# A two-block network on one core: the filter's decay as one channel tile times a factor per position, and the first layer's expert matrices in transfers of 2 MB, 1 MB and 1 MB

## The chip, the cores and the metric

The kernel runs on one core of a Trainium2 chip. The metric is the device time of one execution in microseconds (us); lower is better. Before the change the median of three runs is 2303.51 us (2303.2 to 2305.22).

The core has a tensor engine (PE; its weight loads are listed as PEld), a vector engine (DVE), a scalar engine (ACT), GpSimd (POOL) and SyncE (SP). SP issues nearly all weight loads and POOL the small loads and the stores to DRAM. Each engine works through its own instructions in a fixed order and waits on semaphores for the others. Sixteen DMA engines carry out what SP and POOL issue.

## What is computed

Two blocks follow each other. The first has two layers; each has a token mixer and a mixture of 16 experts, and the first layer runs them on two streams of 256 tokens (context `hc` and latents `x`), the second on the latents alone. The second block is a Hyena layer and an attention layer. What matters here is the expert part and the Hyena filter:

```python
# first block, each layer and stream; cap = 2 * 256 / 16 = 32 tokens per expert
gate, idx = lax.top_k(jnp.swapaxes(aff, 1, 2), cap)
xs = xn[bidx, idx]
hid = silu(einsum('becd,edf->becf', xs, w_gate)) * einsum('becd,edf->becf', xs, w_up)
ys = einsum('becf,efd->becd', hid, w_down) * gate[..., None]      # then added back at idx
# second block: the Hyena filter, L = 256 positions t in [0, 1], 2048 channels
deltas = abs(linspace(MIN_DECAY, MAX_DECAY, 2048))
decay = exp(-t * deltas[None, :])
hf, hb = h[:, :2048] * decay, h[:, 2048:] * decay
k = concatenate([hf, zeros, hb[:0:-1]]); k = k / sum(abs(k))
```

Each expert matrix (gate, up, down) is 1024 x 1024 float32, 4 MB; a layer has 48 of them. `deltas` rises linearly over the channels.

## The kernel before

**Experts.** `route_tokens` picks the tokens and gathers them into `XS`, `experts` goes through the 16 experts: 8 steps of the contraction (k = 0 to 7) for the gate matrix, 8 for up, then silu and the product (ACT, then DVE L874), four transposes on PE (L877), 8 steps for down. In the first layer a step is two matmuls of 64 x 512 side by side (`expert_k`, L841), so a matrix is 16 matmuls, and the profile has two records for each. Expert 0's gate matrix (`early`, tile `psm`) is woven into the gathering (L816). Every fourth expert the results are scattered back by eight matmuls and added to `hc` and `x` (L895, L898).

**Where the matrices land.** `ew` takes a tile for every two k, 1 MB, and issues its load on SP (L915). In the first layer ten buffers rotate: five called `W` (the buffers that every other weight of the kernel uses too), four `W2`, one `W3`. A load waits until PE has used what the buffer held.

**Filter kernels.** Beside the first layer's experts `hkernels` computes the Hyena filter of the second block: `hfilter` (a small network with three sines), then `hkernel` for 16 tiles of 128 channels. Each of them loads `fw4`, its own 128 KB decay tile (L971, POOL) and `dsk`, runs 4 + 4 + 8 small matmuls (L979, L985, L998), multiplies by the decay on DVE (L980) and stores the result to DRAM (`Kd`).

**What follows.** `experts` is followed by the second layer's mixer: the norm of `hc` and `x`, transposes of the normed tiles `xh` (of `hc`) and `og` (of `x`) on PE (L258), then projections in three passes (L111, L112, L113). Its first loads into `W` are `cum` twice, `wT`, and tiles of `w_ada`. The latter belong to a product that is spread through the mixer (`ada`, L205, four matmuls for each 1 MB tile). The five `W` buffers are held back by `wgate`: a tiny POOL copy (L96) reads expert 15's hidden tile before the buffer may be loaded.

**Order.** The program is written in the order above; the tile scheduler then sets the order of the instructions on each engine by its own timeline model, with tiles handed out per pool. So a change of tile sizes can move instructions that it does not mention.

Of the kernel before, what the change touches and what calls it, by code (L numbers as in the profile page):

```python
# [13 lines left out]
OP = mybir.AluOpType  # L14
# [18 lines left out]
class K:  # L33
# [869 lines left out]

    def ew(self, w, k, dma, ns):

        if k % 2 == 0:
            self.ecount += 1
            r = (self.ecount - 1) % 10 if ns == 2 else 11 - self.ecount
            if ns == 1 and r >= 5:
                t = self.T([128, 2, 1024], "W2", 6)  # L910
            elif r < 5:
                t = self.W([128, 2, 1024])
            else:
                t = self.T([128, 2, 1024], *(("W2", 4) if r < 9 else ("W3", 1)))
            dma(t, w[k // 2].rearrange("p (k n) -> p k n", k=2))  # L915
            self.et = t
        return self.et[:, k % 2]


    def hfilter(self):  # L920
# [32 lines left out]
    def hkernels(self):  # L953

        self.fd = self.T([128, 2, 512], "fd")
        self.nc.gpsimd.dma_start(self.fd, self.A["fd"].rearrange("p (k n) -> p k n", k=2))
        with self.pool("filt", tags=("fc", "fz0", "fw1", "fw2", "fa", "fn", "fh")):
            self.hfilter()
        for g in range(16):
            Kt = self.hkernel(g)  # L960
            self.nc.gpsimd.dma_start(self.Kd[g], Kt.rearrange("p a b c -> p (a b c)"))

    def hkernel(self, ct):

        nc, A, T = self.nc, self.A, self.T
        c0 = 128 * ct
        w4 = T([64, 2, 128], "fw4", 1)
        for i in range(2):
            nc.gpsimd.dma_start(w4[:, i], A["hy_fw4_2"][0, :, 2048 * i + c0:2048 * i + c0 + 128])
        dec = T([128, 2, 128], "dec", 1)  # L970
        nc.gpsimd.dma_start(dec, A["decay"][ct].rearrange("p (t n) -> p t n", t=2))  # L971
        dsk = T([1, 128], "dsk", 1)
        nc.gpsimd.dma_start(dsk, A["hy_d_2"][0:1, c0:c0 + 128])
        a = T([128, 2, 2, 128], "ka", 1)
        ab = T([128, 2, 2, 128], "kb", 1)
        ps = self.P([128, 2, 2, 128], "ad")
        for t in range(2):
            for i in range(2):
                nc.tensor.matmul(ps[:, i, t], lhsT=self.h3[:, t * 128:(t + 1) * 128], rhs=w4[:, i], start=True, stop=True)  # L979
        nc.vector.tensor_tensor(a, ps, dec[:, None].to_broadcast([128, 2, 2, 128]), op=OP.mult)  # L980
        nc.vector.memset(a[0:1, 1, 0, :], 0.0)
        nc.vector.scalar_tensor_tensor(ab, a, -1.0, a, op0=OP.mult, op1=OP.max)
        pn = self.P([128, 128], "ad")
        for i in range(4):
            nc.tensor.matmul(pn, lhsT=self.ones, rhs=ab[:, i // 2, i % 2], start=(i == 0), stop=(i == 3))  # L985
        rn = T([128, 128], "krn", 1)
        nc.vector.reciprocal(rn, pn)
        nc.vector.tensor_tensor(ab[:, 0], a[:, 0], a[:, 1], op=OP.add)
        nc.vector.tensor_tensor(ab[:, 1], a[:, 0], a[:, 1], op=OP.subtract)
        abv = ab.rearrange("p i t n -> p (i t) n")  # L990
        nc.vector.scalar_tensor_tensor(abv, abv, 1.0 / 256, rn[:, None, :].to_broadcast([128, 4, 128]), op0=OP.mult, op1=OP.mult)
        nc.vector.tensor_tensor(ab[0:1, 0, 0, :], ab[0:1, 0, 0, :], dsk, op=OP.add)
        Kt = T([128, 2, 2, 128], "Kt", 2)
        ps = self.P([128, 2, 2, 128], "ad")
        for i in range(2):
            for f in range(2):
                for t in range(2):
                    nc.tensor.matmul(ps[:, i, f], lhsT=self.fd[:, t, i * 256 + f * 128:i * 256 + (f + 1) * 128], rhs=ab[:, i, t],  # L998
                                     start=(t == 0), stop=(t == 1))
        self.copy(Kt, ps)  # L1000
        return Kt
# [466 lines left out]
def _constants():  # L1468
    f8 = np.float64
    c = {}  # L1470
    cf = np.zeros((128, 328), np.float32)
    cf[:, 0:128] = np.eye(128)
    cf[:, 128:256] = 1.0 / 256
    for j in range(4):
        for s in range(2):
            cf[32 * j + s, 256 + 2 * j + s] = 1.0
        for e in range(16):
            cf[32 * j + e, 264 + e] = 1.0
        for h in range(4):
            cf[32 * j + h, 280 + 4 * j + h] = -1.0  # L1480
    cf[:, 296:328] = np.arange(1, 33)
    c["cf"] = cf
    t = np.arange(256)
    perm = (t % 64) * 4 + t // 64
    idx = [255 - t, 255 - perm, t, perm]
    cb = np.zeros((128, 384 + 2048), np.float32)
    cb[:, 0:128] = np.eye(128)
    cb[:, 128:256] = np.triu(np.ones((128, 128)), 1)
    cb[:, 256:384] = 1.0
    cum = np.zeros((128, 2, 8, 256), np.float32)  # L1490
    i = np.arange(256)
    for j in range(4):
        mask = np.where(idx[j][:, None] >= idx[j][None, :], 0.0, NEG)
        cb[:, 384 + 512 * j:384 + 512 * (j + 1)] = mask.reshape(2, 128, 256).transpose(1, 0, 2).reshape(128, 512)
        p = (idx[j][:, None] == i[None, :]).reshape(2, 128, 256).transpose(1, 0, 2)
        q = (idx[j][:, None] >= i[None, :]).reshape(2, 128, 256).transpose(1, 0, 2)
        cum[:, :, j] = p
        cum[:, :, 4 + j] = q
    import ml_dtypes
    c["cb"] = cb[:, :384].astype(ml_dtypes.bfloat16)  # L1500
    c["mask"] = cb[:, 384:].astype(ml_dtypes.bfloat16)
    c["cum"] = cum.reshape(128, -1)
    th = 2 * np.pi * (np.outer(t, t) % 256) / 256
    four = np.concatenate([np.cos(th), np.sin(th)], 1)
    c["four"] = four.reshape(2, 128, 512).transpose(1, 0, 2).reshape(128, -1)
    u = np.arange(64)
    ph = 2 * np.pi * (np.outer(u, u) % 64) / 64
    ch = np.zeros((128, 2, 128), f8)
    for g in range(2):
        ch[64 * g:64 * g + 64, 0, 64 * g:64 * g + 64] = np.cos(ph) / 128  # L1510
        ch[64 * g:64 * g + 64, 1, 64 * g:64 * g + 64] = -np.sin(ph) / 128
    c["chan"] = ch.reshape(128, -1)
    wf = 2 * np.pi * ((np.outer(t, 2 * t + 1)) % 1024) / 1024
    fd = np.concatenate([np.cos(wf), np.sin(wf)], 1)
    c["fd"] = fd.reshape(2, 128, 512).transpose(1, 0, 2).reshape(128, -1)

    ws = 2 * np.pi * (np.outer(2 * t - 255, 2 * t + 1) % 2048) / 2048
    c["fe"] = np.concatenate([np.cos(ws[:128]), np.sin(ws[:128])], 1)
    fi = np.concatenate([np.cos(ws).T, np.sin(ws).T], 0) * (2.0 / 512)
    c["fi"] = fi.reshape(4, 128, 256).transpose(1, 0, 2).reshape(128, -1)  # L1520
    tl = np.linspace(0.0, 1.0, 256).astype(np.float32)
    w = (np.float32(2.0 * math.pi) * t.astype(np.float32) / np.float32(256)).astype(np.float32)
    fr = np.linspace(1e-4, 15, 16).astype(np.float32)
    arg = (fr[None, :] * w[:, None]).astype(np.float32).astype(f8)
    z = np.concatenate([tl[:, None].astype(f8), np.cos(arg), -np.sin(arg)], 1)
    c["zpos"] = z.T
    mind, maxd = math.log(1e-2) / 1.5, math.log(1e-2) / 0.3
    deltas = np.abs(np.linspace(mind, maxd, 2048)).astype(np.float32)
    dec = np.exp(-(tl[:, None] * deltas[None, :]).astype(np.float32).astype(f8))
    c["decay"] = dec.reshape(2, 128, 16, 128).transpose(2, 1, 0, 3).reshape(16, 128, 256)  # L1530
    inv = 1.0 / (10000.0 ** (np.arange(0, 64, 2) / 64.0))
    ra = (t // 64)[:, None] * inv[None, :]
    ca = (t % 64)[:, None] * inv[None, :]
    cs = np.concatenate([np.cos(ra), np.cos(ra), np.cos(ca), np.cos(ca)], 1)
    sn = np.concatenate([-np.sin(ra), np.sin(ra), -np.sin(ca), np.sin(ca)], 1)
    rope = np.stack([cs, sn], 0).reshape(2, 2, 128, 128).transpose(2, 0, 1, 3)
    c["rope"] = rope.reshape(128, -1)
    return {k: np.ascontiguousarray(v if v.dtype.itemsize == 2 else v.astype(np.float32)) for k, v in c.items()}


def _layout(inp):
    a = _constants()
    g = {k: np.asarray(v) for k, v in inp.items()}
# [34 lines left out]
    w = g["w_in"]  # L1578
# [7 lines left out]
        a[n] = g[n]  # L1586
    for n in ("w_e_gate", "w_e_up", "w_e_down"):

        a[n] = g[n].reshape(2, 16, 4, 2, 128, 1024).transpose(0, 1, 2, 4, 3, 5).reshape(2, 16, 4, 128, 2048)
    h = g["hy_w_in_2"][0].reshape(8, 128, 4, 16, 128)[:, :, [1, 2, 0, 3]]  # L1590
    a["hyw"] = h.transpose(3, 1, 2, 0, 4).reshape(16, 128, 4096)
    z = g["at_w_in_2"][0][:, 3072:].reshape(8, 128, 4, 4, 128)
# [8 lines left out]
    q, k = g["at_q_g_2"][0], g["at_k_g_2"][0]  # L1601
# [22 lines left out]
```

## Time and profile before

| | |
|---|---|
| median of 3 runs | 2303.51 us |
| the profiled execution | 2303.25 us, of which its span is 2301.1 us |
| PE, DVE, ACT, POOL busy | 91%, 54%, 32%, 8% of the span |
| DMA | 664.09 MB, mean 289 GB/s |
| first layer's experts | about 372 to 883 us of the span |
| second layer's mixer | from there to about 1150 us, DMA at about half |

The page gives the busy share of each engine over the whole span. For this change the stretch of the first layer's experts and the 25 us behind it matter; there both PE and the DMA engines are nearly always busy, and the question at each point is who waits for whom.

### The profile page before, as it was taken

To read this page: it belongs to the slowest core of one execution; us is meant where nothing else is said; L and a number is where in the kernel's file an instruction comes from. 1 tells how busy PE (TensorE), PEld (TensorE's weight loads), DVE (VectorE), ACT (ScalarE), POOL (GpSimd) and SP (SyncE) were. 2 spreads that over 40 slices of the span, in tenths; PEclk is the share of its full clock that TensorE was granted. 3 is DMA by queue.
4 is the path that set the end of the run, shared out by engine and by line. 5 is a ranking of instruction groups with operands and counts; after the bars stand their busy time and mean duration, and the time that the engine had idled before them with its cause. 6 is when DMAs were issued, how large, how long until landed. Compare 5 with 4: busy or idle time off the path is not lost. (4 is left out here: it accounts for less than half of the span.)

```text
span 2301.1 us, 35032 instructions
## 1 busy us (share of the span) xinstructions
PE 2104.5 (91%) x13956; PEld 1414.4 (61%) x13966; DVE 1250.2 (54%) x2533; ACT 738.7 (32%) x1414; POOL 187.6 (8%) x315
## 2 busy tenths in 40 slices
PE   5999988999999998999779889989988999999998
PEld 3775664334333344765446566565657989979786
DVE  3964544333332425844444545444448888775776
ACT  3323432000000004343222222222225555555665
POOL 1000000011001000000000010010001200110100
PEclk9999999999999999999889999999999999999999
DMA  9247563999999997556799999999995555445320
GB/s 351 101 138 303 212 228 129 401 415 413 416 415 415 412 417 287 197 220 217 290 414 419 417 419 416 412 420 416 419 406 177 171 164 174 155 156 181 119 92 19
DMA packets 129587, 664.09 MB, mean 289 GB/s; under 512 B 12666, under 2 KB 23429, under 8 KB 62352
## 3 DMA queue, kind: packets, MB, share of 16 engines
q1 hardware_dynamic: 115616, 602.89, 67.2%
q0 software_dynamic: 13808, 58.96, 6.5%
q8 instruction: 110, 1.80, 0.3%
q14 instruction: 53, 0.43, 0.1%
HBM read 656.56 MB, written 5.24 MB: 288 GB/s over the span
## 5 line engine op out<-in xcount | busy, mean ns | idle before, releaser
L841 PE MATMUL pmm<-W,XS 128*32 128x256 f32 (+1 forms) x3040 | 371.5, 464 | 31.7 <-DMA W<-in_w_e_gate 22.0
L107 DVE TENSOR_TENSOR lo<-W,hi 128x512 fp32r<-128x512 f32 (+1 forms) x420 | 284.0, 681 | 184.4 <-ACT hi L106 181.5
L106 ACT CAST hi<-W 128x512 fp32r<-128x512 f32 (+1 forms) x420 | 255.5, 612 | 348.0 <-PE pmm L112 157.8
L841 PEld LDWEIGHTS pmm<-W,XS 128*32 128x32 f32 (+1 forms) x3040 | 124.2, 120 | 222.6 <-issue 147.1
L107 DVE TENSOR_TENSOR lo<-Wb,hi 128x512 fp32r<-128x512 f32 x160 | 110.7, 693 | 219.9 <-ACT hi L106 217.4
L841 PE MATMUL pmm<-W,hT 128*32 128x256 f32 (+1 forms) x1536 | 185.9, 461 | 26.3 <-DMA W<-in_w_e_down 9.8
L106 ACT CAST hi<-Wb 128x512 fp32r<-128x512 f32 x160 | 98.7, 619 | 339.8 <-PE pmm L112 278.7
L111 PE MATMUL pmm<-hyx,hi 128*128 128x256 f32 x640 | 194.4, 304 | 0.2 <-DVE rtmp L715 0.2
L113 PE MATMUL pmm<-hyx,lo 128*128 128x256 f32 x640 | 182.5, 285 | 0.8 <-DVE lo L107 0.7
L112 PE MATMUL pmm<-hyx,hi 128*128 128x256 f32 x640 | 181.0, 283 | 0.0
L111 PEld LDWEIGHTS pmm<-hyx,hi 128*128 128x128 f32 x640 | 121.3, 190 | 48.9 <-issue 28.2
L111 PE MATMUL pmm<-hyl,hi 128*128 128x256 f32 x512 | 144.6, 283 | 6.2 <-ACT hi L106 4.5
L112 PE MATMUL pmm<-hyl,hi 128*128 128x256 f32 x512 | 144.1, 282 | 0.0
L113 PE MATMUL pmm<-hyl,lo 128*128 128x256 f32 x512 | 142.8, 283 | 0.0
L841 PEld LDWEIGHTS pmm<-W,hT 128*32 128x32 f32 (+1 forms) x1536 | 62.5, 119 | 117.0 <-issue 62.0
L889 DVE TENSOR_TENSOR Y<-pmm,gt 32x512 f32<-32x512 f32 (+1 forms) x128 | 70.9, 554 | 112.8 <-PE pmm L841 111.0
L113 PEld LDWEIGHTS pmm<-hyx,lo 128*128 128x128 f32 x640 | 121.7, 190 | 3.5 <-issue 1.5
L112 PEld LDWEIGHTS pmm<-hyx,hi 128*128 128x128 f32 x640 | 121.7, 190 | 1.0 <-issue 1.0
L205 PE MATMUL pad<-W,cpad 128*32 128x512 f32 x576 | 92.0, 647 | 23.2 <-DMA W<-in_w_ada 16.9
L871 ACT ACTIVATE h<-pmm 128x256 f32<-128x256 f32 (+1 forms) x31 | 15.1, 488 | 270.7 <-PE pmm L841 270.7
L111 PEld LDWEIGHTS pmm<-hyl,hi 128*128 128x128 f32 x512 | 97.3, 190 | 7.6 <-ACT hi L106 5.6
L112 PEld LDWEIGHTS pmm<-hyl,hi 128*128 128x128 f32 x512 | 97.2, 190 | 0.0
(516 smaller groups left out, 3984.5 us busy)
## 6 DMA issues: line engine op xcount, KB each, us to landing
W<-in_w_e_gate SPq DMA_DIRECT2D x128, 1024.0 KB, 13.9
W<-in_w_e_up SPq DMA_DIRECT2D x128, 1024.0 KB, 14.3
W<-in_w_e_down SPq DMA_DIRECT2D x128, 1024.0 KB, 14.5
W<-in_w_ada SPq DMA_DIRECT2D x48, 1024.0 KB, 6.6
W<-in_hyw SPq DMA_DIRECT2D x32, 1024.0 KB, 5.1
Wb<-in_hyw POOLq DMA_DIRECT2D x30, 1024.0 KB, 10.0
W<-in_ada_w SPq DMA_DIRECT2D x24, 1024.0 KB, 5.3
W<-in_at_w_in SPq DMA_DIRECT2D x16, 1024.0 KB, 5.0
```

The costliest lines, as they stand in the source:

```text
L106: self.nc.scalar.copy(hi, w)
L107: self.nc.vector.tensor_tensor(lo, w, hi.bitcast(F32), op=OP.subtract)
L111: first = mm(out, lhsT=l[0], rhs=r[0], start=start, stop=False)
L112: mm(out, lhsT=l[0], rhs=r[1], start=False, stop=False)
L113: mm(out, lhsT=l[1], rhs=r[0], start=False, stop=stop)
L205: nc.tensor.matmul(ps[32 * j:32 * j + 32, :], lhsT=self.cpad[:, blk, k0 + k, :], rhs=wt[:, k, j * 512:(j + 1) * 512], start=(k0 + k == 0), ...
L841: last = self.nc.tensor.matmul(ps[M * j:M * j + M], lhsT=v, rhs=wt[:, j * N:(j + 1) * N], start=(k == 0), stop=(k == 7))
L871: nc.scalar.activation(hv, pgu[0], AF.Silu)
L889: nc.vector.tensor_tensor(Y[s][32 * r:32 * r + 32, c], py[p0:p0 + 32], gt[s][p0:p0 + 32, c], op=OP.mult)
```

## The change

Two things change. First, `decay` for channel tile `ct` is written as the decay of channel tile 0 (`dec`, 128 x 2 x 128) times a factor that depends on position and tile alone (`dect`, one column per tile). Both are loaded once, before the filter network, and the product on DVE becomes two instructions (one for each half of the positions) that multiply by the factor and by `dec`. Second, in the first layer k = 0 to 3 of a matrix come as one transfer of 2 MB into one of two `W2` buffers, and k = 4, 5 and k = 6, 7 as 1 MB each into `W` (five buffers) or, every sixth time, `W3`. The bytes of the ten buffers are the same. The host lays the matrices out so that each transfer is contiguous; in the first layer a partition's row of the 2 MB transfer is 16 KB, of the others 8 KB. The second layer keeps transfers of 1 MB.

```diff
     def ew(self, w, k, dma, ns):
 
-        if k % 2 == 0:
-            self.ecount += 1
-            r = (self.ecount - 1) % 10 if ns == 2 else 11 - self.ecount
-            if ns == 1 and r >= 5:
-                t = self.T([128, 2, 1024], "W2", 6)
-            elif r < 5:
-                t = self.W([128, 2, 1024])
+        per = 4 if ns == 2 and k < 4 else 2
+        if k % per == 0:
+            if per == 4:
+                t = self.T([128, 4, 1024], "W2", 2)
             else:
-                t = self.T([128, 2, 1024], *(("W2", 4) if r < 9 else ("W3", 1)))
-            dma(t, w[k // 2].rearrange("p (k n) -> p k n", k=2))
+                self.ecount += 1
+                if ns == 1:
+                    t = self.T([128, 2, 1024], "W2", 6) if self.ecount <= 6 else self.W([128, 2, 1024])
+                else:
+                    t = self.T([128, 2, 1024], "W3", 1) if self.ecount % 6 == 0 else self.W([128, 2, 1024])
+            dma(t, w[k * 131072:(k + per) * 131072].rearrange("(p k n) -> p k n", p=128, k=per))
             self.et = t
-        return self.et[:, k % 2]
+        return self.et[:, k % per]
...
+        self.dec, self.dect = self.T([128, 2, 128], "dec"), self.T([128, 2, 16], "dect")
+        self.nc.gpsimd.dma_start(self.dec, self.A["decay"].rearrange("p (t n) -> p t n", t=2))
+        self.nc.gpsimd.dma_start(self.dect, self.A["dect"].rearrange("p (t n) -> p t n", t=2))
...
-        dec = T([128, 2, 128], "dec", 1)
-        nc.gpsimd.dma_start(dec, A["decay"][ct].rearrange("p (t n) -> p t n", t=2))
...
-        nc.vector.tensor_tensor(a, ps, dec[:, None].to_broadcast([128, 2, 2, 128]), op=OP.mult)
+
+        for t in range(2):
+            nc.vector.scalar_tensor_tensor(a[:, :, t], ps[:, :, t], self.dect[:, t, ct:ct + 1],
+                                           self.dec[:, None, t].to_broadcast([128, 2, 128]), op0=OP.mult, op1=OP.mult)
...
-    c["decay"] = dec.reshape(2, 128, 16, 128).transpose(2, 1, 0, 3).reshape(16, 128, 256)
+    c["decay"] = dec[:, :128].reshape(2, 128, 128).transpose(1, 0, 2).reshape(128, 256)
+    step = np.exp(-tl[:, None].astype(f8) * (deltas[None, ::128] - deltas[0]).astype(f8))
+    c["dect"] = step.reshape(2, 128, 16).transpose(1, 0, 2).reshape(128, 32)
```

The change moves instructions in three places that the prediction speaks of. The first is SP's order of loads for expert 13 (any expert from 3 on looks alike). Rows name the line, the tile and its source; 128x2048 is 1 MB, 128x4096 is 2 MB, and the waits are on earlier DMAs (DMAHW) and on PE. Before:

```order
L915 DMA W_4219<-in_w_e_gate 128x2048 [waits DMAHW4_49,PE_49]
L915 DMA W_4225<-in_w_e_gate 128x2048 [waits DMAHW5_49,PE_49]
L915 DMA W_4231<-in_w_e_gate 128x2048 [waits DMAHW6_49,PE_49]
L915 DMA W_4237<-in_w_e_gate 128x2048 [waits DMAHW7_49,PE_49]
L915 DMA W<-in_w_e_up 128x2048 [waits DMAHW0_49,PE_49]
L915 DMA W<-in_w_e_up 128x2048 [waits DMAHW1_49,PE_49]
```

and of the changed kernel:

```order
L916 DMA W<-in_w_e_gate 128x2048 [waits DMAHW5_49,PE_49]
L916 DMA W<-in_w_e_gate 128x2048 [waits PE_49]
L916 DMA W_4141<-in_w_e_gate 128x4096 [waits DMAHW7_49,DMAHW1_49,PE_49]
L916 DMA W<-in_w_e_up 128x2048 [waits DMAHW0_49,PE_49]
L916 DMA W<-in_w_e_up 128x2048 [waits PE_49]
L916 DMA W_4164<-in_w_e_up 128x4096 [waits DMAHW4_49,DMAHW2_49,PE_49]
```

The quarters of a matrix came in the order in which PE uses them. Now the two 1 MB pieces (k = 4 to 7) are issued first and the 2 MB piece, which PE uses first, last.

The second is PE's order behind expert 15's last matmuls: the scatter (L895), the `w_ada` steps (L205) and the transposes of the mixer (L258). Before:

```order
L841 MATMUL pmm<-W,hT 64x512 x8
L895 MATMUL psm<-Y,SgT 128x512 x8
L205 MATMUL pad<-W,cpad 32x512 x4
L258 MATMUL pmm<-cf,xh 128x128 x3
L258 MATMUL ptp<-cf,xh 128x128
L205 MATMUL pad<-W,cpad 32x512 x4
L258 MATMUL pmm<-cf,xh 128x128 x9
L258 MATMUL ptp<-cf,xh 128x128 x3
L258 MATMUL psm<-cf,og 128x128 x2
```

and of the changed kernel:

```order
L841 MATMUL pmm<-W_4379,hT 64x512 x4
L895 MATMUL psm<-Y,SgT 128x512 x2
L205 MATMUL pad<-W,cpad 32x512 x4
L895 MATMUL psm<-Y,SgT 128x512 x2
L205 MATMUL pad<-W,cpad 32x512 x4
L895 MATMUL psm<-Y,SgT 128x512 x4
L205 MATMUL pad<-W,cpad 32x512 x4
L258 MATMUL pmm<-cf,xh 128x128 x3
L258 MATMUL ptp<-cf,xh 128x128
L258 MATMUL pmm<-cf,xh 128x128 x9
L258 MATMUL ptp<-cf,xh 128x128 x3
L205 MATMUL pad<-W,cpad 32x512 x4
```

Four `w_ada` steps instead of two now stand ahead of the transposes of `og`; the third and fourth came from the projections behind, where they stood after 7 and 36 matmuls.

The third is SP's order at the same place, where those steps' tiles are loaded. Before:

```order
L367 DMA W<-in_cum 128x2048 [waits DMAHW1_49,Pool_49]
L377 DMA W<-in_wT 128x2x1024 [waits DMAHW2_49,Pool_49]
L200 DMA W<-in_w_ada 128x2048 [waits DMAHW6_49,DMAHW3_49,Pool_49]
L200 DMA W<-in_w_ada 128x2048 [waits DMAHW7_49,DMAHW4_49,Pool_49]
L485 DMA maskb<-in_mask 128x2048 [waits DMAHW5_49,Pool_49]
```

and of the changed kernel:

```order
L377 DMA W<-in_wT 128x2x1024 [waits DMAHW2_49,Pool_49]
L200 DMA W<-in_w_ada 128x2048 [waits DMAHW3_49,Pool_49]
L200 DMA W<-in_w_ada 128x2048 [waits DMAHW5_49,DMAHW4_49,Pool_49]
L377 DMA W<-in_wT 128x2x1024 [waits DMAHW3_49,PE_49]
L200 DMA W<-in_w_ada 128x2048 [waits DMAHW6_49,DMAHW4_49,PE_49]
L485 DMA maskb<-in_mask 128x2048 [waits DMAHW7_49,Pool_49]
```

The second `wT` tile and the third `w_ada` tile moved ahead of `maskb`; both wait for PE, that is for the first and the second `w_ada` step, whose buffers they take. The fourth tile takes the third's.

The filter kernels' matmuls also moved: of the 16 groups of transposes between up and down (L877), 5 had other work directly before them on PE, now 14 have.

## Rows read from the trace of the kernel before

**Rows 1.** The page's DMA issues: KB each, median us from issue to landing, mixer's `w_ada` kind.

```profile
W<-in_ada_w SPq DMA_DIRECT2D x24, 1024.0 KB, 5.3
```

**Rows 2.** Stretches of the experts: us, busy us (instructions), PEclk, DMA share, GB/s.

```profile
450.00:650.00 200.00, 188.69 (x914) 77.01 (x908) 68.25 (x115) 8.28 (x14) 20.48 (x38) 1.00 1.01 416
650.00:850.00 200.00, 186.24 (x924) 77.79 (x924) 64.82 (x110) 8.27 (x14) 19.93 (x37) 0.99 1.01 414
850.00:871.00 21.00, 18.85 (x97) 7.57 (x92) 5.40 (x9) 0.60 (x1) 1.02 (x4) 1.00 1.01 421
```

**Rows 3.** PE's waits from 450 to 850 us: total us, times, longest.

```profile
PE ptp L877 <- DVE h L874: 8.6, 10, 0.9
...
PE pmm L841 <- DMA W<-in_w_e_gate: 0.7, 2, 0.5
```

**Rows 4.** SP's waits from 350 to 930 us: total us, times, longest.

```profile
SPq L915 <- PE pmm L841: 287.2, 147, 6.9
```

**Rows 5.** DMA from 450 to 850 us: packets, MB, share; issues with KB and landing.

```profile
q1 hardware_dynamic: 21807, 158.80, 96.6%
q0 software_dynamic: 3360, 6.89, 4.6%
...
W<-in_w_e_gate SPq DMA_DIRECT2D x52, 1024.0 KB, 17.9
...
dec<-in_decay POOLq DMA_DIRECT2D x15, 128.0 KB, 6.2
```

**Rows 6.** PE at expert 15, in order of time: start, us.

```profile
856.32 7.09 PE L841 MATMUL pmm<-W,XS 128*64 128x512 f32 x32
...
865.71 5.37 PE L841 MATMUL pmm<-W,hT 128*64 128x512 f32 x24 [0.79 <-DVE hT L103]
871.46 1.94 PE L841 MATMUL pmm<-W,hT 128*64 128x512 f32 x8 [0.37 <-DMA W<-in_w_e_down]
```

**Rows 7.** SP's loads as the experts begin, in order of time.

```profile
376.51 0.33 SPq L915 DMA_DIRECT2D W<-in_w_e_down  x1
...
402.49 0.33 SPq L915 DMA_DIRECT2D W<-in_w_e_down  x1
409.30 0.33 SPq L915 DMA_DIRECT2D W<-in_w_e_up  x1
```

**Rows 8.** PE as the experts begin, in order of time.

```profile
381.72 1.08 PE L841 MATMUL psm<-W,XS 128*64 128x512 f32 x4
...
407.32 1.94 PE L841 MATMUL pmm<-W,hT 128*64 128x512 f32 x8
...
430.44 1.11 PE L935 MATMUL pad<-fh,fw 64*64 64x256 f32 x2 [3.39 <-ACT fh L950]
```

**Rows 9.** One stretch with transfers of 4 KB rows (`wT`), columns as in rows 2.

```profile
66.00:72.00 6.00, 6.00 (x28) 4.85 (x27) 5.63 (x12) 1.74 (x3) 0.00 (x0) 1.00 1.01 400
```

**Rows 10.** SP and PE behind the experts, in order of time.

```profile
871.36 2.64 SPq L200 DMA_DIRECT2D W<-in_w_ada  x2
...
877.05 5.80 PE L895 MATMUL psm<-Y,SgT 128*128 128x512 f32 x12 [0.89 <-DVE hc L898]
...
882.77 1.06 PE L205 MATMUL pad<-W,cpad 128*32 128x512 f32 x8
...
884.46 0.55 PE L258 MATMUL pmm<-cf,xh 128*128 128x128 f32 x3 [0.63 <-DVE xh L249]
...
886.17 0.33 SPq L200 DMA_DIRECT2D W<-in_w_ada  x1
...
888.80 0.44 PE L258 MATMUL psm<-cf,og 128*128 128x128 f32 x2 [1.22 <-DVE og L249]
...
894.26 0.80 PE L111 MATMUL pmm<-xhi,hi 128*128 128x512 f32 x1 [1.89 <-ACT xhi L106]
```

**Rows 11.** The third and fourth `w_ada` steps among the projections, in order of time.

```profile
897.97 1.94 PE L205 MATMUL pad<-W,cpad 128*32 128x512 f32 x8
...
905.81 1.06 PE L205 MATMUL pad<-W,cpad 128*32 128x512 f32 x8
```

More of the change, by code (lines that the diff above doesn't have):

```diff
@@ L1587, in _layout @@
     for n in ("w_e_gate", "w_e_up", "w_e_down"):
-        a[n] = g[n].reshape(2, 16, 4, 2, 128, 1024).transpose(0, 1, 2, 4, 3, 5).reshape(2, 16, 4, 128, 2048)
+        v = g[n].reshape(2, 16, 8, 128, 1024).transpose(0, 1, 3, 2, 4)
+        a[n] = np.stack([np.concatenate([v[l, :, :, k:k + m].reshape(16, -1) for k, m in ks], 1)
+                         for l, ks in enumerate((((0, 4), (4, 2), (6, 2)), ((0, 2), (2, 2), (4, 2), (6, 2))))])
     h = g["hy_w_in_2"][0].reshape(8, 128, 4, 16, 128)[:, :, [1, 2, 0, 3]]
```

## The prediction

> **What bounds the kernel now.** I read the page's slices first, to find the stretch that the change touches, then a table of stretches, the waits of PE and of SP there, the DMA view, and the order of time at both ends. From 450 to 871 us the DMA share is 1.01 and the rate 414 to 421 GB/s [rows 2]: the DMA engines always have work. PE is busy 188.69 and 186.24 of 200 us there, and it almost never waits for a weight: 0.7 us in 400, while ten waits for the product h before the transposes cost 8.6 us [rows 3]. SP, on the other hand, waits for PE to hand back buffers, 287.2 us in all [rows 4], and a 1 MB load takes a median 17.9 us to land [rows 5], against 5.3 us for a 1 MB load in the quieter mixers [rows 1]. So the two are balanced: PE sets the pace with its own pauses, and DMA has no reserve to go faster. Only at the last matrix does PE wait for data (0.37 us [rows 6]): the last load lands at about L = 871.4 us, PE ends at t0 = 871.46 + 1.94 = 873.4. A gain needs both: fewer bytes or a higher rate, and fewer pauses of PE.
>
> **The change part by part.** Times are differences to the profiled execution, 2303.25 us (span 2301.1), which is 0.3 below the median of the runs.
>
> *Decay loads.* 16 loads of 128 KB become one, and 16 KB for the factors: 15 x 0.131 - 0.016 = 1.95 MB less. At 415 GB/s that is 4.7 us. By POOL's own queue: its 6.89 MB took 4.6% of 400 us, 18.4 us, of which 15 decay loads (1.97 MB) are 5.3 [rows 5]. I take -5.0 for DMA; the lower end is no gain, if PE doesn't get shorter. On DVE one product becomes two of half the size; DVE is busy a third of the time [rows 2], and what is added stands beside loads.
>
> *PE's pauses.* In the new order 14 groups of transposes instead of 5 have other matmuls before them, which cover the wait for h (0.86 us each [rows 3]): 9 x 0.86 = 7.7 us. The pause of 3.39 us for the first sine [rows 8] gets an up matrix in between. So PE alone could be done up to 11 us sooner. It no longer binds, and the DMA gain can be had; the end is then set by the last landing and what PE has still to do.
>
> *Transfers of 2 MB.* 48 transfers fewer, and half of the bytes in rows of 16 KB. No row shows such a transfer. The nearest pair: rows of 4 KB went at 400 GB/s at a share of 1.01 [rows 9], rows of 8 KB at 415 [rows 2], 3.7% more for a doubling. If the cost is one per row, the next doubling gives half of that, 1.8%, on half of the 482 us: 4.4 us; if it gave the whole step again, 8.9. The other end is none, if 415 to 421 is a ceiling. Being nearer to flat, I take -2.0.
>
> *The start.* From 376.51 to 402.49 SP issues 9 loads of 1 MB before, the next at 409.30 [rows 7]. Now the first 2 MB wait for k = 3 of expert 0's gate (381.72 + 1.08 [rows 8]), but by 402.5 the same 9 MB are issued; the next, 2 MB of up, waits until the first half of down has been used, 407.32 + 8 x 0.44 = 410.9. That is +1.6.
>
> *The end.* The 2 MB piece of a matrix is now issued last, and PE needs it first. When it lands PE has the whole matrix to do, 7.09 us [rows 6], where it had a quarter, 1.94. That is +5.15. Within the stage the same order costs nothing as long as DMA stays full: PE then waits for each matrix, but DMA's end decides.
>
> Together t0 moves by -5.0 - 2.0 + 1.6 + 5.15 = -0.25.
>
> *Behind the experts.* Here the new order adds waits to PE. Take t0 = L + 7.1 as zero. The first `w_ada` tile waits for the POOL copies (which wait for expert 15's h, some 2 us before L) and queues behind the last 2 MB, two `cum` and `wT`; full engines land 1 MB every 2.5 us, so it comes at L + 10, or +2.9, and the second at +5.4. PE: two scatter matmuls, step 1 until +3.9, two more (0.97 each, 5.80 / 6 [rows 10]), step 2 until +6.8, the last four until +10.7; before, the scatter ended at 882.85, +9.45. Step 3's tile takes step 2's buffer: issued at +6.8, landed 5.3 later [rows 1], at +12.1; step 3 ends at +13.1. The 16 transposes of `xh`, 2.4 us, end at +15.5. Step 4's tile takes step 3's buffer, +13.1, and lands at +18.4; step 4 ends at +19.4. Only then come the transposes of `og`, which before began at 888.80, +15.4 [rows 10]: +4.0. What follows up to the first projection (888.80 to 894.26) depends on them and moves along. In return steps 3 and 4 no longer interrupt the projections: -1.94 - 1.06 = -3.0 [rows 11]. This part is +1.0; its ends are -3.0 (the tiles are there in time) and +6 (each landing 2.5 us later, behind one more transfer).
>
> *Sum:* -0.25 + 1.0 = +0.75, forecast **2304 us**. Its own range, from the ends of the 2 MB term and of the last part, is 2298 to 2311.
>
> **The rivals.**
> *A: longer rows raise the rate.* With the whole step of 3.7% on half of the bytes, -8.9 instead of -2.0: 2303.25 + 0.75 - 6.9 = 2297.1, and 2293 if the tiles behind the experts land in time as well. For it: rows of 4 and 8 KB differ [rows 2, 9]. Against it: rates stay between 414 and 421 with 8 KB rows. The Trainium skill ("DMA: Bandwidth & Descriptors", Anatomy of one DMA) puts a fixed cost of about 2 us on each DMA of the POOL path beside its bytes, and its rules for authors ask for large transfers; by that 48 fewer would give 96 us. The trace speaks against paying it one by one: 1.05 MB take 2.5 us of the engines' time in all at 415 GB/s [rows 2], so it is overlapped.
>
> *B: DMA runs dry, slower.* A 2 MB buffer comes back every second matrix: 2 x 10.1 us (4.19 MB at 415 GB/s), of which PE uses it 3.55, the transfer takes 5.05 and the landing adds 2.8: 8.8 us to spare. Before, ten buffers of 1 MB gave 25.3 - 1.8 - 5.3 = 18.2, of which 12.6 were in use (17.9 - 5.3 [rows 1, 5]). When PE turns to other work for longer than 8.8 us within a matrix, SP has nothing to issue. The scatter (8 x 0.97 = 7.8) with a filter kernel beside it (4.2) is 12: 3.2 us lost at three scatters within the stage, +9.6: 2313.6. It decides as soon as the DMA share falls below 1 between 450 and 850. Against it: the two don't always come together, and PE has 11 us fewer of pauses. The skill (same page, Why a DMA increments its semaphore by 16) states that only the full count means that all has landed; so 2 MB are of no use until the last byte, which speaks against this change. No run here shows a 2 MB load.
>
> *C: the saved DMA time is not used* because PE still paces the stage: its pauses move elsewhere (the new order puts some of the filter's steps closer behind each other). Then t0 stays at 873.4 and only the last part counts: 2303.25 + 1.0 = 2304.3.
>
> **How the numbers follow.** Forecast 0.42, A 0.27, B 0.17, C 0.14. What this measurement can tell from no change is 0.2%, 4.6 us, so "same" is 2298.9 to 2308.1. Forecast: 0.05 faster, 0.32 same, 0.05 slower; A: 0.20 faster, 0.07 same; B: 0.03 same, 0.14 slower; C: 0.13 same, 0.01 slower. Together 0.25, 0.55, 0.20. For the range I go down to 2296, which holds most of A, and up to 2312, which leaves out half of B.
>
> **What would show it.** In the changed profile: whether the DMA share stays at 1.01 from 412 us to the last landing (else B) and whether its rate is above 421 GB/s (then A) tell the cases apart. PE should wait for weights some 0.5 us per matrix, none of it before transposes; the last matrix should be 32 records in one piece, 7.1 us, behind a wait for its 2 MB; t0 within 2 us of 873.4. Behind it, steps 3 and 4 of `w_ada` should each be preceded by a wait for `w_ada`, and the first projection should begin about 25 us after t0 instead of 20.9. Wrong would be a t0 that moves by more than 5 us, or no wait for `w_ada` there.

## The result: 1.2% slower, and the profile after

The changed kernel takes 2330.68 us (median; 2328.27 to 2332.54), the kernel before in the same session 2304.36: ratio 1.0116, interval 1.0098 to 1.0134. The forecast of 2304 and its range up to 2312 missed it. The profiled execution (2328.27 us, span 2326.3, before 2301.1) has 25.2 us to explain. First the stretches of the experts, columns as in [rows 2]:

```profile
450.00:650.00 200.00, 179.26 (x873) 77.83 (x871) 69.14 (x125) 7.08 (x12) 17.41 (x33) 0.97 0.99 400
650.00:850.00 200.00, 186.84 (x902) 78.88 (x902) 63.52 (x113) 8.28 (x14) 13.79 (x26) 0.98 0.98 399
850.00:871.00 21.00, 16.30 (x76) 5.56 (x72) 3.44 (x5) 1.18 (x2) 0.00 (x0) 1.00 1.00 420
```

From 450 to 850 us the DMA share, 1.01 before, is below 1, and the rate fell from 416 and 414 to 400 and 399 GB/s: the sign that the prediction had named for rival B. Slices of 20 us say where:

```profile
510.00:530.00 20.00, 20.00 (x74) 6.69 (x70) 4.95 (x9) 0.60 (x1) 1.04 (x2) 1.00 1.01 410
530.00:550.00 20.00, 17.65 (x95) 8.22 (x96) 9.03 (x16) 0.58 (x1) 2.11 (x4) 1.00 0.92 362
550.00:570.00 20.00, 15.71 (x90) 8.16 (x88) 6.20 (x13) 1.18 (x2) 2.11 (x4) 1.00 0.94 366
570.00:590.00 20.00, 20.00 (x104) 8.20 (x102) 7.18 (x13) 0.60 (x1) 2.11 (x4) 1.00 0.99 387
...
630.00:650.00 20.00, 16.61 (x74) 5.84 (x72) 9.21 (x17) 0.00 (x0) 1.54 (x3) 1.00 0.96 383
650.00:670.00 20.00, 19.32 (x84) 7.86 (x84) 5.83 (x10) 1.77 (x3) 1.61 (x3) 1.00 0.85 334
670.00:690.00 20.00, 20.00 (x104) 8.18 (x102) 6.06 (x10) 0.60 (x1) 1.07 (x2) 1.00 1.00 404
770.00:790.00 20.00, 17.59 (x68) 6.51 (x68) 8.95 (x15) 0.60 (x1) 1.07 (x2) 1.00 0.97 392
790.00:810.00 20.00, 19.27 (x94) 7.41 (x92) 6.43 (x12) 0.58 (x1) 1.04 (x2) 1.00 0.89 344
```

There are three dry spells, each behind a scatter (experts 3, 7 and 11 end at 504, 638 and 768 us). Against 415 GB/s they lack 2.60, 2.48 and 1.88 MB (for the first: (53 + 49 + 28) x 20 us), 6.96 MB in all, or 16.8 us. The first begins only at 530 us, when its scatter is nearly done, in filter-kernel steps that wait 1.62, 2.37 and 1.93 us for DVE. PE in the second one, in order of time:

```profile
638.37 1.16 PE L990 MATMUL pad<-kb,cf 128*128 128x128 f32 x8
639.36 1.88 PE L895 MATMUL psm<-Y,SgT 128*128 128x512 f32 x4
643.65 1.12 PE L895 MATMUL psm<-Y,SgT 128*128 128x512 f32 x2 [2.41 <-DVE hc L898]
644.71 5.37 PE L841 MATMUL pmm<-W,XS 128*64 128x512 f32 x24
...
665.04 1.94 PE L841 MATMUL pmm<-W,XS 128*64 128x512 f32 x8
```

From 638.37 to 666.98 PE does two matrices, 14.18 us of work, in 28.61: it is away for 14.4 us with the scatter, a filter kernel and a wait for `hc`. SP meanwhile has no free buffer:

```profile
636.76 11.97 SPq L916 DMA_DIRECT2D W<-in_w_e_down  x3
650.12 12.59 SPq L916 DMA_DIRECT2D W<-in_w_e_gate  x3
664.10 3.25 SPq L916 DMA_DIRECT2D W<-in_w_e_up  x2
```

From the first load of one matrix to the first of the next it takes 13.4 and 14.0 us, where 4.19 MB need 10.1. SP's waits for PE from 350 to 930 us (287.2 before [rows 4]), then PE's waits from 450 to 850 us [rows 3], the last fence of the kernel before:

```profile
SPq L916 <- PE pmm L841: 405.9, 132, 10.3
```

```profile
PE pad L1003 <- DVE kb L997: 13.3, 6, 2.4
PE pad L990 <- DVE kb L987: 5.8, 3, 1.9
PE psm L895 <- DVE hc L898: 4.8, 2, 2.4
...
PE pmm L841 <- DMA W<-in_w_e_up: 1.0, 1, 1.0
...
PE pmm L841 <- DMA W<-in_w_e_gate: 0.4, 1, 0.4
```

```profile
PE pad L985 <- DVE kb L982: 3.4, 2, 1.7
PE pad L998 <- DVE kb L992: 3.1, 4, 1.6
```

The waits for h before the transposes are gone, as forecast; in their place the filter kernels' steps wait for DVE, 19.1 us instead of 6.5. For weights PE waits only 1.4 us in these 400, the last time at 482.74 us: it isn't held up by data, it holds up the loads. The end of the experts and what follows [rows 6, 10]:

```profile
872.53 7.09 PE L841 MATMUL pmm<-W,XS 128*64 128x512 f32 x32 [2.77 <-DMA W<-in_w_e_up]
882.40 7.09 PE L841 MATMUL pmm<-W,hT 128*64 128x512 f32 x32 [1.27 <-DMA W<-in_w_e_down]
895.60 1.93 PE L205 MATMUL pad<-W,cpad 128*32 128x512 f32 x8 [3.34 <-DMA W<-in_w_ada]
906.72 1.06 PE L205 MATMUL pad<-W,cpad 128*32 128x512 f32 x8 [1.76 <-DMA W<-in_w_ada]
913.34 1.94 PE L205 MATMUL pad<-W,cpad 128*32 128x512 f32 x8 [3.66 <-DMA W<-in_w_ada]
920.77 0.50 PE L111 MATMUL pmm<-xhi,hi 128*128 128x512 f32 x1 [1.89 <-ACT xhi L106]
```

The last piece, 2 MB, is there at 882.40 (before, the last 1 MB at 871.46: +10.9), PE then has a whole matrix to do, t0 = 889.49 (before 873.40: +16.1), and the first projection begins 31.3 us behind it (before 20.9: +10.4). Behind that the kernel is 1.3 us shorter. 16.1 + 10.4 - 1.3 = 25.2.

### The profile page after: what moved, and what is told of

Same layout as the page of the kernel before. It is cut to its first block, busy times and chain, and to the rows that moved or that the text cites. A ratio compares the mean times of both kernels' runs of the same rounds, so it can differ in the third digit from the quotient of the medians.

```text
span 2326.3 us, 34877 instructions
## 1 busy us (share of the span) xinstructions
PE 2119.7 (91%) x13956; PEld 1429.0 (61%) x13966; DVE 1252.1 (54%) x2549; ACT 738.1 (32%) x1414; POOL 179.0 (8%) x301
## 4 chain that ended last, share of the span: by engine, by line
PE 71%; DMA 14%; DVE 9%; ACT 3%; issue 2%; POOL 1%; SPq 0%; DVEq 0%; ACTq 0%; POOLq 0%
PE pmm L841 18%; PE pmm L111 11%; PE pmm L112 10%; PE pmm L113 10%; DMA W<-in_w_e_up 4%; DMA W<-in_w_e_gate 3%; DMA W<-in_w_e_down 3%; PE pad L205 3%; DMA W<-in_w_ada 3%; DVE lo L107 2%; PE psm L895 1%; PE pad L1003 1%; PE ptp L1042 1%; PE pmm L816 1%; DMA W<-in_ada_w 1%
## 5 line engine op out<-in xcount | busy, mean ns | idle before, releaser
L205 PE MATMUL pad<-W,cpad 128*32 128x512 f32 x576 | 92.0, 650 | 31.5 <-DMA W<-in_w_ada 24.4
## 6 DMA issues: line engine op xcount, KB each, us to landing
W<-in_w_e_up SPq DMA_DIRECT2D x96, 1024.0 KB, 12.9
```

The lines of the kernel that those rows point to most:

```text
L205: nc.tensor.matmul(ps[32 * j:32 * j + 32, :], lhsT=self.cpad[:, blk, k0 + k, :], rhs=wt[:, k, j * 512:(j + 1) * 512], start=(k0 + k == 0), ...
```

## The experiments

Ratios are to the kernel before on the same chip, with their 95% interval. "Rate" is from 450 to 650 and from 650 to 850 us.

**Each half of the change alone.** `decay_only` has only the decay part of the diff.

> The kernel before with the decay change alone; the matrices still come as 1 MB in ten buffers. Theory D (the DMA engines set the pace of the experts, so 1.95 MB less are 4.7 us): 2299.7 us, t0 (end of expert 15's last matmul) at 868.7 instead of 873.4. Rival P (PE paces there, the saved DMA time isn't used): 2304, t0 at 873. Rival V (the second instruction on DVE lengthens the chain that PE waits for in the filter kernels, and the loss of the changed kernel is partly from that): 2310 or more.

Measured: 2301.37 us, 0.9986 (0.9975 to 0.9996), so 3.2 us faster. Its last stretch and its last matrix:

```profile
850.00:871.00 21.00, 18.86 (x95) 7.24 (x93) 4.54 (x8) 0.60 (x1) 1.19 (x5) 1.00 0.97 396
```

```profile
863.98 7.09 PE L841 MATMUL pmm<-W,hT 128*64 128x512 f32 x32 [0.79 <-DVE hT L103]
```

The DMA engines run out of work before PE does (share 0.97), and the last matrix waits for `hT`, no longer for data. t0 = 871.07, 2.3 us earlier, between D and P: DMA's gain is used until PE becomes the bound. V falls. Of the versions that leave no work out, this is the one that beats both kernels.

`big_only` has only the new `ew` and the layout.

> The kernel before with the 2 MB, 1 MB, 1 MB transfers alone; 16 decay loads and one DVE product as before. Theory B (the DMA engines run dry behind the scatters, because a 2 MB buffer leaves too little reserve, and the end and the w_ada waits cost what the changed kernel shows): the loss of the changed kernel plus the 4.7 us that the decay loads take, 2330.7 + 4.7 = 2335 us, rate from 450 to 850 near 400 GB/s. Rival V (the decay's second DVE instruction carries the loss): 2304 to 2311 and a rate of 414.

Measured: 2339.91 us, 1.0152 (1.0136 to 1.0167), rate 400 and 399. The transfers carry the whole loss; the 5 us above the forecast stay open. But the spells don't lie behind every scatter here:

```profile
610.00:630.00 20.00, 16.41 (x82) 7.96 (x80) 7.62 (x13) 0.60 (x1) 2.69 (x5) 0.91 0.94 371
770.00:790.00 20.00, 17.59 (x74) 5.84 (x68) 7.94 (x14) 0.00 (x0) 0.51 (x1) 1.00 1.01 415
790.00:810.00 20.00, 19.32 (x89) 7.98 (x90) 4.99 (x8) 1.77 (x3) 0.57 (x1) 1.00 1.01 425
```

```profile
781.67 1.12 PE L895 MATMUL psm<-Y,SgT 128*128 128x512 f32 x2 [2.41 <-DVE hc L898]
```

The third scatter has the same order on PE and the same pause as the second and third of the changed kernel (776.39 to 804.99 us less two matrices, 14.4 us), and it leaves no dip. A dip of 371 GB/s from 610 to 630 us has no scatter near it, but a wait of 3.59 us of a filter step for DVE. One expert before this third scatter PE had last waited for a weight, at 736.42 us; in the changed kernel the last such wait, at 482.74, lies 156 and 286 us before its second and third scatter.

**The end and the order behind it.** `after_last1`:

```diff
+            self.lastm = e == 15
...
-        per = 4 if ns == 2 and k < 4 else 2
+        per = 4 if ns == 2 and k < 4 and not self.lastm else 2
...
+                dma(t, w[:524288].rearrange("(p k n) -> p k n", p=128, k=4)[:, k:k + 2])
```

The last line takes the two halves out of the 2 MB that lie together in DRAM.

> The changed kernel, but the last expert's three matrices come as four transfers of 1 MB each in order of use. PE's order behind the experts is then the old one again (steps 3 and 4 of w_ada behind the transposes of og). Theory: the end is 1.94 us behind the last landing instead of 7.09 (-5.15) and the first projection begins about 21 us after t0 instead of 31.3 (-10.4): together -15.5, so 2315 us; the dry spells behind the three scatters stay, rate 400 GB/s from 450 to 850. Rival (the whole loss is made within the stage, and what is late behind it is late anyway, since all later loads queue behind): -5 or less, 2326 or more.

Measured: 2317.8 us, 1.0046 (1.003 to 1.0061), 12.9 below the changed kernel (9.3 between the two profiled spans); the spells stay, rate 398 and 396. PE at the end:

```profile
886.45 1.94 PE L841 MATMUL pmm<-W,hT 128*64 128x512 f32 x8 [0.34 <-DMA W<-in_w_e_down]
...
900.26 1.06 PE L205 MATMUL pad<-W,cpad 128*32 128x512 f32 x8 [1.42 <-DMA W<-in_w_ada]
...
910.71 0.80 PE L111 MATMUL pmm<-xhi,hi 128*128 128x512 f32 x1 [1.89 <-ACT xhi L106]
```

With the old order the first projection comes 22.3 us behind t0 instead of 31.3 (-9.0, expected -10.4). The end has 1.94 us behind the last landing as expected, but t0 is only 1.1 earlier, not 5.15: the last expert's twelve pieces share six buffers, and the last lands 4 us later (rate 395 from 850 to 871 us).

**The scatters.** The same edit in the changed kernel and in the one before:

```diff
-            if r == 3:
+            if e == 15 or (ns == 1 and r == 3):
```

> The changed kernel with the first layer's scatters behind experts 3, 7 and 11 left out (the results of those experts are not added back; only the last scatter stands). All loads, matmuls of the experts and filter kernels remain. Theory B (the DMA engines run dry because PE is away with a scatter for longer than a 2 MB buffer can wait): the three spells are gone, the rate from 450 to 850 is 412 or more, t0 near 873 and the time 2314 us (2330.7 less the 16.8 us of the three spells). Rival F (the filter kernels' matmuls and their waits for DVE hold PE and cause the spells): rate stays near 400, 2327 or more.

> The kernel before with the same three scatters left out. The DMA engines set its pace already and don't run dry behind a scatter, so 23 us less work on PE bring next to nothing: 2302 to 2305 us. Rival P (PE paces the experts): up to 23 us faster, 2281.

Measured: 2307.35 us, 1.0027 (1.0014 to 1.0041), and 2301.98, 0.9997 (0.9988 to 1.0007). The changed kernel gains 23 us, the one before nothing. The stretches of the first:

```profile
450.00:650.00 200.00, 179.03 (x923) 81.37 (x924) 64.62 (x119) 8.86 (x15) 19.06 (x36) 0.98 1.01 417
650.00:850.00 200.00, 178.16 (x865) 76.41 (x865) 56.17 (x100) 7.10 (x12) 12.20 (x23) 0.95 1.01 418
```

The spells are gone, with all filter kernels in place: F falls as a cause by itself, though their steps wait for DVE even longer here (29.0 us from 450 to 850). t0 is 872.13 (873 expected). The rest of the gain lies behind it: the first projection comes 28.5 us behind t0 instead of 31.3.

**The filter kernels.** Again the same edit in both, in `hkernels`:

```diff
-            Kt = self.hkernel(g)
+            Kt = self.hkernel(0) if g == 0 else Kt
```

> The changed kernel with one filter kernel computed and stored 16 times, 15 left out (their matmuls, DVE products and fw4 loads are gone). Beside a scatter PE then has only the scatter's 7.9 us and its wait for hc (2.4 us): 10.3 against the 8.8 us that a 2 MB buffer leaves. Theory B with a threshold: 1.5 us lost at each of three scatters, 4.5 instead of 16.8; with the end and the w_ada waits as in the changed kernel, and 1 MB of fw4 less (2.4 us): 2330.7 - 12.3 - 2.4 = 2316 us, rate from 450 to 850 at 412 or more with shallow dips behind the scatters. Rival (the scatter alone empties the queue, whatever is beside it): rate 400 and 2328.

> The kernel before with one filter kernel computed and stored 16 times. The DMA engines pace it: 15 loads of fw4 (1.0 MB) and of decay (1.97 MB) less are 7.2 us at 415 GB/s, so 2297 us, if PE doesn't become the bound; the rate rises towards 421 (the value of before where no filter kernel runs), which would give up to 6 us more, 2291. If only PE's work counted, 15 x 4.2 = 63 us less: 2241.

Measured: 2308.5 us, 1.0025 (1.0015 to 1.0035), and 2294.27, 0.996 (0.9946 to 0.9975). From 650 to 850 us, changed kernel first:

```profile
650.00:850.00 200.00, 167.15 (x704) 59.29 (x702) 31.51 (x46) 6.52 (x11) 0.00 (x0) 0.95 1.01 424
```

```profile
650.00:850.00 200.00, 164.17 (x694) 47.26 (x692) 30.91 (x45) 5.94 (x10) 0.00 (x0) 1.00 1.01 421
```

Neither theory had this right: a scatter with nothing beside it (pauses of 10.3 us) leaves no dip at all. So in the changed kernel it takes both, scatters and filter kernels. PE waits 46.9 us for weights from 450 to 850 us here, so it isn't behind when a scatter comes; then 10.3 us fit, 1.5 more than the 8.8 to spare. `before_1filt` came between its two figures, with the DMA share at 1.01: the DMA engines set the pace of the kernel before.

**Fewer buffers of 1 MB.** The kernel before with eight (two `W2`) and six (no `W2`) rotating buffers; the edit for six:

```diff
-            r = (self.ecount - 1) % 10 if ns == 2 else 11 - self.ecount
+            r = (self.ecount - 1) % 6 if ns == 2 else 11 - self.ecount
...
-                t = self.T([128, 2, 1024], *(("W2", 4) if r < 9 else ("W3", 1)))
+                t = self.T([128, 2, 1024], "W3", 1)
```

> The kernel before with eight buffers of 1 MB instead of ten. To spare are 8 x 2.53 - 1.8 - 5.3 = 13.1 us, more than the 12 us of a scatter with a filter kernel beside it. Theory B with its threshold: no dry spell, rate 414 from 450 to 850; only the start is later, since 2 MB less are loaded before expert 0 (5.1 us; with six buffers it was 3.84 MB less by 430 us): 2309.5 us. Rival (the loss grows evenly with each buffer taken away): half of what six buffers cost, with dry spells behind the scatters of half the depth, 2315.

> The kernel before with six rotating buffers of 1 MB instead of ten (five W, one W3); transfers stay at 1 MB and in order of use. By the reckoning of the prediction, six buffers leave 6 x 2.53 - 1.8 - 5.3 = 8.1 us to spare, about as little as the two 2 MB buffers (8.8). Theory B (the reserve decides): dry spells behind the three scatters as in the changed kernel, about 16 us lost, 400 GB/s from 450 to 850, 2320 us; the end and the part behind the experts as before. Rival S (the size or the order of the 2 MB transfers decides, not the reserve): within 5 us of before, 2304 to 2309, rate 414.

Measured: 2319.01 us, 1.0076 (1.0057 to 1.0095), and 2326.17, 1.0097 (1.0082 to 1.0113). Slices of the one with eight, then of the one with six:

```profile
410.00:430.00 20.00, 19.22 (x82) 6.24 (x84) 6.05 (x12) 1.48 (x3) 0.00 (x0) 0.91 0.73 274
670.00:690.00 20.00, 19.08 (x100) 8.27 (x98) 6.92 (x12) 1.17 (x2) 2.68 (x5) 1.00 1.00 398
790.00:810.00 20.00, 18.41 (x96) 7.65 (x97) 6.81 (x12) 0.59 (x1) 0.55 (x1) 1.00 0.96 365
```

```profile
530.00:550.00 20.00, 19.32 (x104) 9.59 (x102) 6.85 (x12) 1.18 (x2) 2.68 (x5) 1.00 0.91 349
670.00:690.00 20.00, 19.32 (x100) 8.47 (x100) 6.60 (x12) 1.17 (x2) 2.68 (x5) 1.00 0.89 347
790.00:810.00 20.00, 18.41 (x80) 6.00 (x80) 2.76 (x4) 1.18 (x2) 0.00 (x0) 1.00 0.99 398
```

With 1 MB transfers in order of use, spells behind the scatters appear once buffers are few, so S falls; they are about half as deep as the changed kernel's. But the sharp threshold falls too: eight buffers, which were to have no spell, have a shallow one. The loss isn't even either: eight buffers cost 15.8 us, six 21.3. And the start costs more than forecast: from 390 to 430 us eight buffers got 322 and 274 GB/s, where ten had 372 and 397, so 3.5 MB or 8.3 us less (5.1 expected). With six the spells make up only some 9 of the 24 us by which t0 is later; the start and the thinner reserve in between make up the rest.

**The size of the transfer or its readiness.** `after_halves` fills each 2 MB buffer with two transfers; `after_halves_rev` swaps the two lines:

```diff
-            dma(t, w[k * 131072:(k + per) * 131072].rearrange("(p k n) -> p k n", p=128, k=per))
+            src = w[k * 131072:(k + per) * 131072].rearrange("(p k n) -> p k n", p=128, k=per)
+            if per == 4:
+                dma(t[:, :2], src[:, :2])
+                dma(t[:, 2:], src[:, 2:])
+            else:
+                dma(t, src)
```

> The changed kernel with each 2 MB buffer filled by two transfers of 1 MB (k = 0, 1 and k = 2, 3); buffers and their return as in the changed kernel. Theory B (the late return of a 2 MB buffer decides): the spells stay, rate near 400 from 450 to 850; at the end the last landing leaves PE a little less to do (k = 2 to 7, 5.3 us instead of 7.1) and only step 3 of w_ada stands ahead of og: 2330.7 - 1.8 - 3.7 = 2325 us. Rival S (one transfer of 2 MB, usable only when all of it has landed, decides): rate back to 412 or more, 2310.

> The changed kernel with each 2 MB buffer filled by two transfers of 1 MB (rows of 8 KB), k = 2, 3 first and k = 0, 1 last. PE's order stays nearly that of the changed kernel, since PE can't begin a matrix before its last half has landed. Theory L (what costs is that PE can't begin before all 2 MB are there, and the order of its other work that follows from that, not the size of a transfer): dry spells as in the changed kernel, rate near 400 from 450 to 850, four w_ada steps ahead of og, 2325 to 2332 us. Rival S (two transfers of 1 MB are in themselves better than one of 2 MB, by their rows or their number in flight): like the halves in order of use, 2307, rate 410.

Measured: 2306.76 us, 1.0018 (1.0008 to 1.0027), and 2336.6, 1.0148 (1.0131 to 1.0165). The stretches in the order of use, then swapped:

```profile
450.00:650.00 200.00, 189.63 (x929) 82.94 (x929) 75.37 (x137) 8.71 (x15) 19.55 (x37) 0.98 1.01 409
650.00:850.00 200.00, 183.76 (x893) 73.89 (x892) 59.08 (x104) 7.77 (x14) 11.70 (x22) 1.00 1.01 412
```

```profile
450.00:650.00 200.00, 181.66 (x868) 78.82 (x866) 69.25 (x125) 7.69 (x13) 17.43 (x33) 0.96 0.97 393
650.00:850.00 200.00, 183.78 (x874) 77.60 (x872) 64.08 (x113) 7.69 (x13) 13.79 (x26) 0.97 0.96 382
```

The first result went against my expectation and is near rival S: with the same 2 MB buffers, returned after the same step (k = 3), most of the loss is gone. The second is near L (2325 to 2332), against S: the same transfers of 1 MB, only with k = 0, 1 last, lose 6 us more than the changed kernel, with dips in nine slices of 20 us between 530 and 850 us. So neither the size of a transfer nor the return of the buffer alone decides; what differs is when PE can begin a matrix. The Trainium skill ("DMA: Bandwidth & Descriptors", Why a DMA increments its semaphore by 16) says that only the full count means that all has landed. The ends of the traces agree: the changed kernel does the last matrix in one piece of 32 records behind one wait (1.27 us at 882.40), the halves do the up matrix before in 8 and 24 records with a wait before each (1.25 us at 861.16, 0.47 at 863.57).

But PE hardly pays for this as a wait: 1.4 us for weights from 450 to 850 us in the changed kernel, none in the swapped version. What PE waits for there are the filter kernels' products on DVE, 19.1 and 24.5 us, against 7.3 in the halves. So the later beginning seems to work through PE's order of instructions, which the scheduler derives from it: in the halves it spreads the scatter in twos and fours between quarters of matrices, in the swapped version it keeps nearly the changed kernel's blocks. That this order is what costs is argued, not shown: no run changes it alone.

**The large piece last.** k = 0 to 3 come as two transfers of 1 MB, k = 4 to 7 as one of 2 MB, with the layout to match:

```diff
-        per = 4 if ns == 2 and k < 4 else 2
+        per = 4 if ns == 2 and k >= 4 else 2
```

> The changed kernel with the halves exchanged: k = 0, 1 and k = 2, 3 as 1 MB each, k = 4 to 7 as one transfer of 2 MB, so the large piece is used last. Theory L (what the changed kernel loses is that PE can't start a matrix before its 2 MB have landed, which are issued last, so PE is late by most of a matrix and has no reserve when a scatter comes): PE starts with the 1 MB pieces, the spells shrink to what the two halves of 1 MB showed (5 us instead of 17), the end has 3.55 us of PE behind the last landing instead of 7.09; w_ada still stands in front: 2330.7 - 11 - 3.5 = 2316 us. Rival R (only the return of the 2 MB buffer every second matrix counts, which is the same for either half): spells as in the changed kernel, 2330.7 - 3.5 = 2327, rate 400.

Measured: 2333.41 us, 1.0141 (1.0115 to 1.0166), rate 401 and 394. L's 2316 is far off; R has the rate right and misses the time by 6 us. PE can begin a matrix with 1 MB here, and the loss stays, which speaks against the beginning alone. It isn't a clean test: the scheduler also mixed gate, up and down matrices on PE, and SP waited 65.8 us for earlier transfers of up.

## Why the prediction was wrong, step by step

*What failed* are two steps. The first and larger is "Within the stage the same order costs nothing as long as DMA stays full: PE then waits for each matrix, but DMA's end decides". DMA didn't stay full, and PE didn't wait: 1.4 us for weights from 450 to 850 us, where 0.5 us per matrix would be some 20. PE with its other work set the pace, SP waited for buffers, and t0 moved by +16.1 instead of -0.25. The second is the part behind the experts, +1.0 with ends of -3 and +6: it measures +9.1.

The mechanism of the first was on the page as rival B, with its place and its sign, at 0.17 and +9.6 us; it measures +16.8. B's pause was 12 us (scatter and filter kernel); it is 14.4 in two of the three spells, since the scheduler put scatter matmuls in a block and PE waits 2.41 us for `hc`. With 12.8, 14.4 and 14.4 us against the same 8.8 to spare, B gives 4.0 + 5.6 + 5.6 = 15.2. That the sum nearly fits is luck: spell by spell 6.3, 6.0 and 4.5 us are lost. A pause of 10.3 cost nothing, nor did the one of 14.4 in `big_only`; in the halves a pause of 13.2 us cost 3 us at the first scatter and nothing at the third. So what is to spare isn't a fixed 8.8; it seems to depend on how far PE is behind when the pause comes. I held against B that PE would have 11 us fewer of pauses; the waits for h did go, but the filter steps' waits for DVE grew by 12.6, the place that rival C had named.

The granted clock of PE was a little lower from 450 to 850 us, 0.97 and 0.98 instead of 1.00 and 0.99 [rows 2]; in the slice from 490 to 510 us, at 0.83, one matrix took 9.13 us instead of 7.09. No run separates what that adds. It isn't enough for a spell: without scatters the clock was 0.98 and 0.95 and the DMA engines stayed full, and with six buffers it was 1.00 and they didn't.

*Decay loads*, -5.0: 3.2 us alone, because PE becomes the bound at the end. In the changed kernel all of it seems to count for DMA: 16.8 - 4.7 leaves 12.1, and the last landing is 10.9 late.

*Transfers of 2 MB*, -2.0: where DMA is full on both sides and little other traffic disturbs, in the two runs with one filter kernel, the rate is 424 against 421 GB/s, 0.7% or 3.4 us of 482, from one trace each. Right in sign, the forecast somewhat small; A's whole step (1.8% on the whole) isn't there.

*The end*, +5.15: as predicted, 32 records in one piece behind the wait for its 2 MB; 10.9 + 5.15 = 16.1 = the shift of t0.

*Behind the experts*, +4.0 - 3.0: the place was right, w_ada's tiles for steps 1, 3 and 4, the size was not. The tiles came 6.1, 17.2 and 23.9 us behind t0, where I had 2.9, 12.1 and 18.4. The last 2 MB landed at 882.40 and the first `w_ada` tile, 4.19 MB later, at 895.60: 318 GB/s, where I took 415 at once behind full engines. They weren't full, in stretches of 2 us:

```profile
880.00:882.00 2.00, 0.66 (x4) 0.42 (x4) 1.11 (x2) 0.00 (x0) 0.53 (x4) 1.00 0.57 139
882.00:884.00 2.00, 1.60 (x8) 0.75 (x10) 0.00 (x0) 0.00 (x0) 0.00 (x0) 1.00 0.81 291
```

The POOL copies come at 880.49 us, some 2 us before the landing as I had it, and SP's first load behind them at 880.68; that is too late to keep the engines busy (before: copies at 864.28, 7.2 us before the landing). From there the chain is as forecast: the tiles of steps 3 and 4 land 5.5 us behind their issue. Measured +10.4 - 1.3. Over all runs the order decides this term: where steps 3 and 4, or one of them, stand behind the transposes of `og`, the first projection comes 20.9 to 23.0 us behind t0 (eight kernels), where both stand ahead of its end, 28.5 to 31.6 (six).

*The start*, +1.6: from 370 to 450 us the DMA engines moved 320 GB/s instead of 327, 0.56 MB or 1.3 us less, near the forecast, though PE ended expert 1 5.4 us earlier than before.

## What to carry to other kernels

Where DMA and PE are balanced, count what one buffer holds back: a larger transfer means PE can start later and gives the buffer back later, and the reserve must still outlast PE's longest absence (here a scatter with a filter kernel beside it, 14 us). How much of the reserve is there when the absence comes depends on how far PE is behind, so a single figure for it misleads. The same bytes of buffers in fewer, larger tiles are a smaller reserve; the larger transfers gave 0.7% here and the dry spells cost five times that. Look at the consumer's order of instructions as well, since a scheduler may change it with the sizes. And look at the end: the piece that lands last should be the one with the least work behind it.

## What was not expected of the hardware

Only that the filter kernels' small loads seem to cost the stream more than their bytes: without 15 filter kernels the kernel before moved 421 GB/s, all bytes counted, where it had 414 to 416 [rows 2], at a DMA share of 1.01 in both. No run separates these loads from the rest of what was left out.
